# An embedding lookup with position add: hand-placed semaphores, 24 tile slots and stores in halves

## The chip, the cores and the metric

The kernel runs on one core of one Trainium2 chip. The metric is the device time in microseconds of one execution, as the median of ten. Its profile is one execution recorded by the hardware profiler.

## The reference

```python
batch, seq_len, vocab_size, d_model = 32, 512, 50000, 512
token_embed = embedding_table[indices]          # 32 x 512 rows of 512 float32
return (token_embed + position_embed).astype(np.float32)
```

For each of 32 sequences, 512 rows of 2048 bytes are picked from a table of 50,000 rows by an index, and row s of the position table is added to the row at place s. The result is 33.5 MB, and as much is gathered, so the work is almost wholly movement: about 67 MB through the DMA engines and one addition for each element.

## The kernel before

One sequence of 512 places is laid over 128 partitions, four places (k = 0 to 3) to a partition: place s = 4p + k stands in partition p. A whole sequence is then a tile of 128 x 4 x 512 float32, 1 MB, and each partition's part of it is 8192 contiguous bytes of the output.

The stages, by line:

- SyncE loads the indices of sequence 0 in their final layout (line 49, `idx0`), all indices with a sequence in each partition (line 51, `idx_raw`), and the position table in four parts (line 56, `pos_sb`).
- VectorE casts the indices to float32 (line 68), TensorE turns them with four small transposes (line 73), and VectorE casts them back into `idx_t` (line 75), which has the indices of all sequences with the place in the partition.
- ScalarE copies the position parts into PSUM (line 79, `pos_ps`).
- For each sequence `chunk` takes a tile, and for each k GpSimd issues an indirect DMA (line 88) that gathers 128 table rows, 256 KB, by one column of indices. VectorE adds the position part in place (line 94). When all parts of a tile are there SyncE stores it (line 97).

Sequences 0, 1 and 31 are cut into four tiles of one part with a store of 256 KB each; sequences 2 to 5 and 30 into two tiles with stores of 512 KB; the others are one tile with a store of 1 MB. That makes 46 stores and 128 gathers. The order on each engine is the order of this loop: GpSimd's queue holds only gathers after its first few instructions, VectorE's the additions, SyncE's the loads and then the stores.

The tile framework places all semaphores and waits. Its data pool has 20 tiles, each of the largest size, 8 KB a partition. It gives software DMAs (the gathers) eight semaphores in turn and hardware DMAs (loads and stores) eight others, so a gather waits for the eighth gather before it, and a store for the eighth hardware DMA before it. An instruction that needs more than one wait gets a semaphore instruction ahead of it. At the end of the program, at the launch line 132, SyncE waits for every one of these semaphores in ten semaphore instructions and a drain, and then all engines meet in a barrier.

Of the kernel before, what the change touches and what calls it, by code (L numbers as in the profile page):

```python
# [1 line left out]

# [4 lines left out]

P = 128
K = 4
BUFS = 20  # L10


@with_exitstack
def kernel(
    ctx: ExitStack,
    tc: tile.TileContext,
    indices: bass.AP,
    embedding_table: bass.AP,
    position_embed: bass.AP,
    out: bass.AP,  # L20
):

    nc = tc.nc
    f32 = mybir.dt.float32
    i32 = mybir.dt.int32
    add = mybir.AluOpType.add

    B, S = indices.shape
    V, D = embedding_table.shape
    assert S == P * K and B == 32  # L30
    assert V < (1 << 24), "an index passes through float32"


    idx_words = indices.bitcast(i32)
    idx_first = idx_words[0].rearrange("(p w) -> p w", p=P)
    out_rows = out.rearrange("b (p k) d -> b p k d", k=K)
    pos_rows = position_embed.rearrange("(p k) d -> p k d", k=K)
    table = embedding_table[:, :]

    const = ctx.enter_context(tc.tile_pool(name="const", bufs=1))  # L40
    data_pool = ctx.enter_context(tc.tile_pool(name="data", bufs=BUFS))
    psum = ctx.enter_context(
        tc.tile_pool(name="psum", bufs=1, space=bass.MemoryType.PSUM)
    )

    idx0 = const.tile([P, 2 * K], i32)
    nc.sync.dma_start(out=idx0[:], in_=idx_first)
    idx_raw = const.tile([B, S, 2], i32)  # L50
    nc.sync.dma_start(
        out=idx_raw[:], in_=idx_words.rearrange("b (s w) -> b s w", w=2)
    )
    pos_sb = [const.tile([P, D], f32, name=f"pos_sb{k}") for k in range(K)]
    for k in range(K):
        nc.sync.dma_start(out=pos_sb[k][:], in_=pos_rows[:, k, :])


    ones = const.tile([B, B], f32)
    nc.gpsimd.memset(ones[:], 1.0)  # L60
    ident = const.tile([B, B], f32)
    nc.gpsimd.affine_select(  # L62
        out=ident[:], in_=ones[:], pattern=[[-1, B]],
        compare_op=mybir.AluOpType.is_equal, fill=0.0, base=0,
        channel_multiplier=1,
    )
    idx_f = const.tile([B, P, K], f32)
    nc.vector.tensor_copy(  # L68
        out=idx_f[:].rearrange("b p k -> b (p k)"), in_=idx_raw[:, :, 0]
    )  # L70
    turned = psum.tile([P, K, B], f32)
    for k in range(K):
        nc.tensor.transpose(turned[:, k, :], idx_f[:, :, k], ident[:])  # L73
    idx_t = const.tile([P, K, B], i32)
    nc.vector.tensor_copy(out=idx_t[:], in_=turned[:])  # L75

    pos_ps = [psum.tile([P, D], f32, name=f"pos_ps{k}") for k in range(K)]
    for k in range(K):
        nc.scalar.copy(out=pos_ps[k][:], in_=pos_sb[k][:])  # L79

    def chunk(b, parts):
        at = 0
        for n in parts:
            data = data_pool.tile([P, n, D], f32, tag="data")
            for j in range(n):
                k = at + j
                where = idx0[:, 2 * k : 2 * k + 1] if b == 0 else idx_t[:, k, b : b + 1]
                nc.gpsimd.indirect_dma_start(  # L88
                    out=data[:, j, :],
                    out_offset=None,  # L90
                    in_=table,
                    in_offset=bass.IndirectOffsetOnAxis(ap=where, axis=0),
                )
                nc.vector.tensor_tensor(  # L94
                    out=data[:, j, :], in0=data[:, j, :], in1=pos_ps[k][:], op=add
                )
            nc.sync.dma_start(out=out_rows[b][:, at : at + n, :], in_=data[:])  # L97
            at += n

    for b in range(B):  # L100
        if b <= 1 or b == B - 1:
            chunk(b, (1, 1, 1, 1))
        elif b <= 5 or b == B - 2:
            chunk(b, (2, 2))
        else:
            chunk(b, (K,))


# [1 line left out]
_INS = ['indices', 'embedding_table', 'position_embed']  # L110
_OUTS = [((32, 512, 512), 'float32')]


# [23 lines left out]
```

## Time and profile before

| what | value |
|---|---|
| median of 10 runs | 184.56 us (184.51 to 184.64) |
| the profiled execution's own time | 184.57 us |
| its span, first to last instruction | 182.9 us |
| GpSimd busy | 121.7 us (67%), 134 instructions |
| VectorE busy | 87.3 us (48%), 130 instructions |
| gathers on GpSimd | 128, about 946 ns each |
| additions on VectorE | 128, 687 ns each |
| DMA moved | 68.33 MB, mean 374 GB/s over the span |

How to read it: a line of the page with one digit for each fortieth of the span gives the busy share in tenths. [...] data moves afterwards on the 16 DMA engines, which serve the gathers' queue (q0, software) and the loads' and stores' queue (q1, hardware) alike. SyncE computes nothing and only issues and waits; where an answer shows "SPq" it is SyncE's sequencer. The trace also has a record for each DMA packet, with start, duration and size, and for many of the semaphores' updates; where the text says packet records or landings, these are meant.

### The profile page before, as it was taken

Reading aid. Unit: us, or ns where it says so; the run is one execution under the profiler, and the core shown is the slowest. Engines: PE = TensorE matmul, PEld = TensorE weight load, DVE = VectorE, ACT = ScalarE, POOL = GpSimd, SP = SyncE. Lnnn points to the kernel's source line nnn. Section 1 sums busy time; section 2 is a strip of 40 time slices with the busy share of each in tenths; the row PEclk is TensorE's granted clock in tenths of the full one; section 3 lists DMA queues with packets and bytes.
Section 4 is the critical chain, followed back from the end, with each engine's and each line's share of the span. In section 5 each row is a group of like instructions: output and inputs, shape, how many; then the busy total and the mean of one; then the engine's idle time right before and its main releaser. Section 6 shows DMA issues by size and latency. Waiting matters only on the chain.

```text
span 182.9 us, 480 instructions
## 1 busy us (share of the span) xinstructions
PE 0.7 (0%) x4; PEld 0.6 (0%) x4; DVE 87.3 (48%) x130; ACT 3.6 (2%) x5; POOL 121.7 (67%) x134
## 2 busy tenths in 40 slices
PE   0100000000000000000000000000000000000000
PEld 0000000000000000000000000000000000000000
DVE  0163645545545454464746464464547465445300
ACT  2500000000000000000000000000000000000000
POOL 4777777777777777777777777778777777750000
DMA  4889999999999999999999999999999999999900
GB/s 129 319 258 369 358 395 390 418 398 410 400 391 398 403 407 410 406 416 404 418 413 412 417 410 419 409 414 419 416 420 407 417 414 417 411 409 417 396 15 0
DMA packets 17635, 68.33 MB, mean 374 GB/s; under 512 B 3008, under 2 KB 3008, under 8 KB 14560
## 3 DMA queue, kind: packets, MB, share of 16 engines
q0 software_dynamic: 10240, 33.56, 48.0%
q1 hardware_dynamic: 7392, 34.74, 46.5%
q14 instruction: 3, 0.02, 0.0%
HBM read 34.74 MB, written 33.55 MB: 373 GB/s over the span
## 4 chain that ended last, share of the span: by engine, by line
DMA 47%; POOL 22%; issue 18%; POOLq 3%; DVE 2%; SPq 1%; DVEq 1%
DMA data<-in_embedding_table_dram,idx_t 39%; POOL data L88 22%; DMA out_dram<-data 7%; POOLq L88 3%; DVE data L94 2%; SPq L97 1%; DMA idx<-in_indices_dram 1%; DVEq L94 1%
## 5 line engine op out<-in xcount | busy, mean ns | idle before, releaser
L88 POOL DMA_INDIRECT data<-in_embedding_table_dram,idx_t x124 | 117.2, 945 | 38.3 <-issue 38.0
L94 DVE TENSOR_TENSOR data<-data,pos_ps 128x512 f32<-128x512 f32 x128 | 86.6, 687 | 79.8 <-issue 54.1
L88 POOL DMA_INDIRECT data<-in_embedding_table_dram,idx x4 | 4.0, 994 | 2.4 <-DMA idx<-in_indices_dram 1.5
L79 ACT COPY pos_ps<-pos_sb 128x512 f32<-128x512 f32 x4 | 2.4, 589 | 4.2 <-DMA pos_sb<-in_position_embed_dram 4.0
L68 DVE CAST idx_f<-idx_raw 32x512 f32<-32x512 int32 x1 | 0.4, 415 | 3.8 <-DMA idx_raw<-in_indices_dram 3.8
L79 ACT ACT_TABLE_LOAD x1 | 1.3, 1283 | 0.8 <-PEq L121 0.8
L75 DVE CAST idx_t<-turned 128x128 int32<-128x128 f32 x1 | 0.3, 291 | 0.8 <-PE turned L73 0.8
L73 PE MATMUL turned<-ident,idx_f 32*128 32x32 f32 x4 | 0.7, 297 | 4.4 <-DVE idx_f L68 4.4
L73 PEld LDWEIGHTS turned<-ident,idx_f 32*128 32x128 f32 x4 | 0.6, 206 | 4.4 <-issue 4.4
L121 POOL MEMSET const-float32-0.0<- 128x1 f32 x1 | 0.1, 105 | 0.3 <-issue 0.3
L60 POOL MEMSET ones<- 32x32 f32 x1 | 0.1, 114 | 0.3 <-POOLq L121 0.3
L62 POOL TENSOR_SCALAR_AFFINE_SELECT ident<-ones 32x32 f32<-32x32 f32 x1 | 0.2, 202 | 0.1
L121 POOL MEMSET const-uint8-127<- 128x1 uint8 x1 | 0.1, 122 | 0.0
L121 POOL MEMSET const-bfloat16-1.0<- 128x1 bf16 x1 | 0.1, 116 | 0.0
L121 POOL MEMSET const-float32-1.0<- 128x1 f32 x1 | 0.1, 108 | 0.0
## 6 DMA issues: line engine op xcount, KB each, us to landing
out_dram<-data SPq DMA_DIRECT2D x24, 1024.0 KB
out_dram<-data SPq DMA_DIRECT2D x10, 512.0 KB
out_dram<-data SPq DMA_DIRECT2D x12, 256.0 KB
data<-in_embedding_table_dram,idx_t POOLq DMA_INDIRECT x124
pos_sb<-in_position_embed_dram SPq DMA_DIRECT2D x4, 256.0 KB
idx_raw<-in_indices_dram SPq DMA_DIRECT2D x1, 128.0 KB
data<-in_embedding_table_dram,idx POOLq DMA_INDIRECT x4
idx<-in_indices_dram SPq DMA_DIRECT2D x1, 4.0 KB
```

The lines of the kernel that those rows point to most:

```text
L60: nc.gpsimd.memset(ones[:], 1.0)
L62: nc.gpsimd.affine_select(out=ident[:], in_=ones[:], pattern=[[-1, B]], compare_op=mybir.AluOpType.is_equal, fill=0.0, base=0, channel_mul ...
L68: nc.vector.tensor_copy(out=idx_f[:].rearrange("b p k -> b (p k)"), in_=idx_raw[:, :, 0])
L73: nc.tensor.transpose(turned[:, k, :], idx_f[:, :, k], ident[:])
L75: nc.vector.tensor_copy(out=idx_t[:], in_=turned[:])
L79: nc.scalar.copy(out=pos_ps[k][:], in_=pos_sb[k][:])
L88: nc.gpsimd.indirect_dma_start(out=data[:, j, :], out_offset=None, in_=table, in_offset=bass.IndirectOffsetOnAxis(ap=where, axis=0),)
L94: nc.vector.tensor_tensor(out=data[:, j, :], in0=data[:, j, :], in1=pos_ps[k][:], op=add)
L97: nc.sync.dma_start(out=out_rows[b][:, at : at + n, :], in_=data[:])
L121: nc = _bacc.Bacc("TRN2", target_bir_lowering=False, num_devices=1)
```

## The change

The computation, the layout, the number of gathers and additions, and the order of gathers and additions stay. What changes:

- All instructions stand in one critical section, in which the framework places no waits; the kernel allocates its own semaphores and writes each wait. Entering it, every engine waits for a no-operation of SyncE; leaving it, SyncE signals the engines and collects a signal from each.
- The pool of 20 tiles becomes 24 fixed slots of one sequence each (`slots`), so sequence b uses slot b mod 24. Sequences 24 to 31 wait, at their first gather, for the stores of sequence b - 24.
- The gathers use 16 semaphores in turn (`LANES`), so a gather waits for the sixteenth before it.
- Each addition waits for its gather's semaphore, and those of sequence 0 also for the position copy. A store waits for one counter of additions, `s_add`, and no longer for an earlier DMA.
- Sequences 1 to 30 are stored in two halves of 512 KB; sequences 0 and 31 in four quarters of 256 KB. That makes 68 stores. The gathers of a sequence fill one slot, whatever the cut of its stores.
- SyncE ends with one wait for all stores of sequences 8 to 31 (`s_rest`). GpSimd ends with a drain inside the section.

The diff, cut to its core:

```diff
-BUFS = 20
+SLOTS = 24
+LANES = 16
+HALVES = (2, 2)
+QUARTERS = (1, 1, 1, 1)
...
+    slots = [sbuf(f"slot{n}", [P, K, D], f32) for n in range(SLOTS)]
...
+    stores = []
+    for b in range(B):
+        parts = QUARTERS if b in (0, B - 1) else HALVES
+        at = 0
+        for n in parts:
+            stores.append((b, at, n))
+            at += n
...
+    def rounds(g):
+        return 16 * (g // LANES + 1)
+
+    with tc.tile_critical(no_gpsimd_drain=True):
...
+        nc.gpsimd.wait_ge(s_first, 16)
+        for g in range(B * K):
+            b, k = divmod(g, K)
+            if g == K:
+                nc.gpsimd.wait_ge(s_idx, 1)
+            if b >= SLOTS and k == 0:
+                done = sum(1 for x in stores if x[0] == b - SLOTS)
+                nc.gpsimd.wait_ge(s_out[b - SLOTS], 16 * done)
+            where = idx0[:, 2 * k : 2 * k + 1] if b == 0 else idx_t[:, k, b : b + 1]
+            ins = nc.gpsimd.indirect_dma_start(
+                out=slots[b % SLOTS][:, k, :],
...
+            ).then_inc(s_gather[g % LANES], 16)
+            if g >= LANES:
+                ins._wait_ge(s_gather[g % LANES], rounds(g - LANES))
+        nc.gpsimd.drain()
...
+        for g in range(B * K):
+            b, k = divmod(g, K)
+            if b == 0:
+                nc.vector.wait_ge(s_ps, k + 1)
+            part = slots[b % SLOTS][:, k, :]
+            nc.vector.tensor_tensor(
+                out=part, in0=part, in1=pos_ps[k][:], op=add
+            )._wait_ge(s_gather[g % LANES], rounds(g)).then_inc(s_add, 1)
...
+        rest = 0
+        for b, at, n in stores:
+            done = s_out.get(b, s_rest)
+            rest += done is s_rest
+            nc.sync.dma_start(
+                out=out_rows[b][:, at : at + n, :],
+                in_=slots[b % SLOTS][:, at : at + n, :],
+            )._wait_ge(s_add, b * K + at + n).then_inc(done, 16)
+        nc.sync.wait_ge(s_rest, 16 * rest)
```

## The prediction

> **What bounds the kernel now.** I read the page's slices first, then the groups and queues, then a table of busy times by stretch, the gathers late in the order of time, and last the SyncE instructions of the launch line.
>
> The slices of the span (4.57 us each) and the DMA queues, from the page:
>
> ```profile
> DVE  0163645545545454464746464464547465445300
> ...
> POOL 4777777777777777777777777778777777750000
> DMA  4889999999999999999999999999999999999900
> GB/s 129 319 258 369 358 395 390 418 398 410 400 391 398 403 407 410 406 416 404 418 413 412 417 410 419 409 414 419 416 420 407 417 414 417 411 409 417 396 15 0
> ...
> q0 software_dynamic: 10240, 33.56, 48.0%
> q1 hardware_dynamic: 7392, 34.74, 46.5%
> ```
>
> The 16 DMA engines are full from the fifth slice to the 38th. q0 (gathers) and q1 (loads and stores) took 94.5% of the span, 172.8 us of all 16 engines. Then come two slices of nothing: 15 and 0 GB/s.
>
> The table by stretch (per engine busy us and instructions, then clock, DMA share, GB/s) shows the same closer:
>
> ```profile
> 36.00:44.00 8.00, 0.00 (x0) 0.00 (x0) 4.49 (x7) 0.00 (x0) 6.02 (x7) 1.00 1.03 408
> 48.00:60.00 12.00, 0.00 (x0) 0.00 (x0) 5.93 (x10) 0.00 (x0) 9.26 (x10) 1.00 1.00 394
> 60.00:80.00 20.00, 0.00 (x0) 0.00 (x0) 10.76 (x16) 0.00 (x0) 15.12 (x17) 1.00 1.01 408
> 80.00:160.00 80.00, 0.00 (x0) 0.00 (x0) 42.81 (x64) 0.00 (x0) 59.96 (x65) 1.00 1.02 414
> ...
> 174.60:182.90 8.30, 0.00 (x0) 0.00 (x0) 0.00 (x0) 0.00 (x0) 0.00 (x0) 1.00 0.00 0
> ```
>
> Share 1.02 is full: one packet per engine at every moment. From 174.6 to 182.9 nothing moves and nothing computes: 8.3 us, 4.5% of the span.
>
> GpSimd, in the order of time, with its gap in brackets:
>
> ```profile
> 159.70 0.95 POOL L88 DMA_INDIRECT data<-in_embedding_table_dram,idx_t  x1 [0.30 <-issue]
> 160.95 0.95 POOL L88 DMA_INDIRECT data<-in_embedding_table_dram,idx_t  x1 [0.30 <-issue]
> 162.20 0.95 POOL L88 DMA_INDIRECT data<-in_embedding_table_dram,idx_t  x1 [0.30 <-issue]
> ```
>
> A gather costs GpSimd 1.25 us, whatever it waits for. From the second gather (4.16) 126 steps of 1.25 us end at 161.66; the last one starts at 162.20. So all of its waits, for tiles and for the eighth gather back, cost 0.54 us in the whole run. GpSimd is a second bound a little below the DMA engines: 512 KB per 1.25 us is 419 GB/s, where the DMA moves 414.
>
> The launch line on SyncE (count, then minimum/median/maximum ns, first and last start):
>
> ```profile
> L132 SPq EVENT_SEMAPHORE  x12: 1/353/699, 175.7 to 182.8; - x12
> L132 SPq DRAIN  x3: 7/7/7, 182.0 to 182.3; - x3
> ```
>
> These are the framework's closing waits, ten instructions with up to two semaphores each, for every DMA lane. The last store's semaphore was complete at 174.53 by the trace's landings, yet SyncE reaches its drain at 182.04. In between most records lie 0.70 us apart, although the semaphores were satisfied. The final barrier takes 182.09 to 182.86. The last chain is thus: DMA engines full to 174.5, SyncE's slow wait list to 182.04, barrier.
>
> **What the Trainium skill says.** "DMA: Bandwidth & Descriptors", Rules for kernel authors, asks for 1 MiB or more per DMA for the most bandwidth. The trace agrees weakly: by its packet records a store packet of 8192 B (1 MB stores) takes 311 ns, of 4096 B (512 KB stores) 159 ns, of 2048 B 84 ns, so 26.3, 25.8 and 24.4 B/ns. The same page, Queues, rings and completion order, says that each engine takes turns between queue rows packet by packet. That fits a gather packet of 4096 B whose time varies with its neighbour: 170 ns from 28 to 46 us beside 4096 B stores, 164 from 100 to 160 beside 8192 B ones. [...] in the trace the first instructions follow the opening barrier by 0.07 us, branch included.
>
> **The change, part by part.** The sum is made against the profiled execution, 184.57 us with a span of 182.86, so 1.71 outside; it is within 0.01 of the median 184.56.
>
> 1. Entry. Each engine now runs one more branch that waits for a SyncE no-operation. By the 0.07 us above and one semaphore hop of some 0.05 (the barrier's release at 0.69 is seen at 0.74), about 0.2 us, on the path of the first index load. Bounds 0.1 and 0.6.
>
> 2. Gathers. 128 as before, now allowed 16 in flight and 24 tile slots instead of 20 tiles. All they can win on GpSimd is 0.54 us, and the DMA engines have no room for it: 0. The cover is that saturation: a gather lands 8.3 us after its issue (159.70 to 168.04), nearly seven in flight, so the limit of eight hardly held. Bounds: -0.5, and +0.5 if deeper queues cost.
>
> 3. Waits folded into instructions. DVE and SyncE lose separate semaphore instructions of 0.02 us when satisfied. Both engines have slack (DVE 48% busy). 0.
>
> 4. Stores in halves. Before: 12 of 256 KB, 10 of 512 KB, 24 of 1 MB, each of 128 rows of one packet: 1536 x 84 + 1280 x 159 + 3072 x 311 ns = 1288 us, over 16 engines 80.5. After: 8 of 256 KB and 60 of 512 KB: 1024 x 84 + 7680 x 159 = 1307 us, 81.7. That is +1.2, straight onto the bound. 22 more stores with 16 completion writes of 9 ns each add 22 x 9 ns = +0.2. The gather packets of the 24 sequences stored whole before (24 x 4 x 64 = 6144) may each take 6 ns more beside shorter stores: 6144 x 6 / 16 = +2.3. But part of that difference is drift along the run: at 46 to 60 us, beside 8192 B stores, they took 175. I take half, +1.1. Sum +2.5; bounds +1.2 (packet sums alone, some of it hidden) and +3.7. SyncE issues 22 more stores of 0.33 us, one per 2.5 us of data: covered. Sequence 1 in halves starts its stores a little later and the last sequence stays in quarters: 0.
>
> 5. Tail. Ten wait instructions go. SyncE waits once for all stores from sequence 8 on (the earlier ones are proved by slot reuse), then runs seven instructions (semaphore, drain, two semaphore waits, no-operation, branch, drain) and the same barrier. Before, from the last landing to the end: 182.86 - 174.53 = 8.33 us. After, if they run at their ordinary 0.02 to 0.07 us: landing seen 0.1, exit with two hops 0.5, barrier 0.77 = 1.4. The trace doesn't say why SyncE went slow from 167.3 on; if it does so again each instruction costs 0.70. I take 2.0, mostly fast with one slow step: -6.3. Bounds -6.9 and -2.0.
>
> Sum: 184.57 + 0.2 + 2.5 - 6.3 = 181.0 us. The DMA end moves from 174.5 to 177.2, the end of the span comes 2.0 later at 179.2.
>
> **The rivals.**
>
> - Slow SyncE follows (other side). Its 0.70 us steps began at 167.3, before the closing list, in ordinary stores and waits, so they may belong to SyncE late in the run and not to the list. Then eight instructions after the last landing cost 8 x 0.70 = 5.6, the barrier 0.77: 177.2 + 6.4 + 1.7 = 185.3. It decides when a step exceeds about 0.6 us. For it: the start before the list. Against: earlier SyncE waits took 0.017 us, and the run ends with fast steps after 182.
> - The half stores cost all they can: the rate stays at the 394 to 403 GB/s of the stretches from 28 to 60 us and never climbs to 414. For the 115 us up to 161 us 2.7% is 3.1 instead of the 2.5, at worst 5: 183.5 with the tail of 2.0. For it: 408 and 394 in the table. Against: the rate rises along the run with the stores' size unchanged.
> - Deeper queues win: early gathers no longer bunch, gather packets keep 164 ns, the tail takes its 1.4 us: 184.57 + 0.2 + 1.2 - 6.9 - 0.5 = 178.6. Against: share 1.02 leaves nothing to fill; only the first 20 us have some 3.7 us of idle share, and GpSimd's pace sets those.
> - The lanes don't do what they say: if GpSimd holds its own limit on outstanding gathers, 16 lanes act as eight. That changes nothing in the sum, 181.0.
>
> **How the numbers follow.** The forecast has a chance of 0.56 (lanes without effect included), deeper queues 0.08, costly halves 0.12, slow SyncE 0.20, and 0.04 for something that holds GpSimd up. Predicted 181.0. The range 178.6 to 185.1 holds the first three cases and the lower part of the slow one, leaving about 0.06 below and 0.14 above. A measurement here can tell 0.2%, 0.4 us, from no change. Faster takes the first three cases but for a sliver: 0.75; the slow case spreads about 185.3, with a quarter of it in the band: same 0.05, slower 0.20.
>
> **What would show it.** In the changed profile: the last DMA bytes near 177 and less than 2.5 us from there to the end of the span (step 5); store packets of 159 ns throughout q1 and gather packets between 164 and 170 (step 4); gathers still 1.25 us apart (step 2); the first index load at about 1.0 us instead of 0.81 (step 1). It is wrong if SyncE's last instructions again stand 0.7 us apart, or if the rate in the middle falls under 400 GB/s.

## The result and the profile after

The changed kernel takes 183.51 us (median of 8 runs, 183.41 to 183.59). The kernel before, measured beside it, takes 184.57. The ratio is 0.9942, with a 95% interval of 0.9934 to 0.9951, so the change wins 1.06 us. The forecast was 181.0, a win of 3.6: the direction was right, the size was not, and two terms of the sum were wrong by more than the whole effect.

The profiled execution of the changed kernel took 183.49 us, with a span of 182.3. First the slices and the queues of its page (a slice is 4.56 us here):

```profile
DMA  4889999999999999999999999999999999999800
GB/s 129 302 245 364 357 367 405 415 407 418 417 416 420 413 417 417 416 417 417 421 420 417 417 415 416 416 421 418 417 417 417 414 406 415 419 415 416 333 2 0
...
q1 hardware_dynamic: 10560, 34.74, 47.5%
q0 software_dynamic: 10240, 33.56, 46.9%
```

Then the same stretches as before, with the columns of the table by stretch (busy us per engine and instructions, clock, DMA share, GB/s):

```profile
48.00:60.00 12.00, 0.00 (x0) 0.00 (x0) 6.39 (x10) 0.00 (x0) 9.02 (x10) 1.00 1.03 417
60.00:80.00 20.00, 0.00 (x0) 0.00 (x0) 11.00 (x16) 0.00 (x0) 15.12 (x17) 1.00 1.03 416
80.00:160.00 80.00, 0.00 (x0) 0.00 (x0) 43.54 (x64) 0.00 (x0) 60.50 (x65) 1.00 1.03 417
...
172.00:174.60 2.60, 0.00 (x0) 0.00 (x0) 0.00 (x0) 0.00 (x0) 0.00 (x0) 1.00 0.16 61
174.60:182.30 7.70, 0.00 (x0) 0.00 (x0) 0.00 (x0) 0.00 (x0) 0.00 (x0) 1.00 0.00 0
```

Two things are to be seen. The rate in the middle did not fall with stores of half the size: it rose, from 394 to 417 GB/s at 48 to 60 us and from 414 to 417 at 80 to 160. The DMA engines are almost done at 172: their share in the next stretch is 0.16, where it was 0.70 in the kernel before:

```profile
172.00:174.60 2.60, 0.00 (x0) 0.00 (x0) 0.00 (x0) 0.00 (x0) 0.00 (x0) 1.00 0.70 269
```

Their last bytes move at 172.95, before at 174.54. And yet the stretch with nothing in it is still there, and longer: 182.3 - 172.95 = 9.3 us, before 8.3.

What fills it are SyncE's own records, on the line of the critical section (L89) and on the launch line (L189). The columns are count, then minimum/median/maximum ns, then first and last start in us:

```profile
L89 SPq EVENT_SEMAPHORE  x3: 17/1170/1400, 173.9 to 176.6; - x3
L89 SPq NOP  x2: 4/8/13, 0.8 to 178.7; - x2
...
L189 SPq DRAIN  x3: 15/700/704, 179.4 to 182.2; - x3
L189 SPq EVENT_SEMAPHORE  x2: 5/10/15, 182.2 to 182.3; - x2
```

The list is short now: from the last bytes on, SyncE has eleven records up to the final barrier's last. The first three, up to 173.96, are quick. The next ones take 1.17, 1.40, 0.70 and 0.70 us, or stand 0.7 to 2.6 us apart, until 182.2; then three in a row pass in 0.05 us. In the trace of before the slow steps ended at 181.99, and they had begun at 167.3 among the stores (SyncE's store line from 165 us on):

```profile
L97 SPq DMA_DIRECT2D out_dram<-data x5: 332/556/706, 165.7 to 174.3; - x5
L97 SPq EVENT_SEMAPHORE  x4: 17/695/700, 166.0 to 172.9; - x4
```

The DMA engines finished 1.6 us earlier, and SyncE became quick within 0.25 us of the same moment.

The balance of the two profiled executions: last bytes -1.6, from there to the end of the span +1.0, outside the span 1.71 to 1.2, -0.5. Sum -1.1, the measured change.

### The profile page after: what moved, and what is told of

The parts are those of the page before. It is cut to its first block, busy times and chain, and to the rows that moved or that the text cites. A ratio compares the mean times of both kernels' runs of the same rounds, so it can differ in the third digit from the quotient of the medians.

```text
span 182.3 us, 421 instructions
## 1 busy us (share of the span) xinstructions
PE 0.7 (0%) x4; PEld 0.6 (0%) x4; DVE 88.3 (48%) x130; ACT 3.6 (2%) x5; POOL 121.9 (67%) x134
## 4 chain that ended last, share of the span: by engine, by line
POOL 63%; issue 23%; DMA 5%; DVE 2%; POOLq 1%; SPq 0%
POOL slot L116 63%; DMA slot<-in_embedding_table_dram,idx_t 4%; DVE slot L146 2%; DMA idx<-in_indices_dram 1%; POOLq L124 1%; POOLq L114 0%; SPq L189 0%; SPq L89 0%
## 5 line engine op out<-in xcount | busy, mean ns | idle before, releaser
L116 POOL DMA_INDIRECT slot<-in_embedding_table_dram,idx_t x124 | 117.2, 945 | 37.8 <-issue 37.8
L146 DVE TENSOR_TENSOR slot<-slot,pos_ps 128x512 f32<-128x512 f32 x128 | 87.6, 687 | 77.1 <-issue 39.4
L116 POOL DMA_INDIRECT slot<-in_embedding_table_dram,idx x4 | 4.1, 1027 | 2.4 <-DMA idx<-in_indices_dram 1.5
```

The source lines that it names most:

```text
L116: ins = nc.gpsimd.indirect_dma_start(out=slots[b % SLOTS][:, k, :], out_offset=None, in_=table, in_offset=bass.IndirectOffsetOnAxis(ap=whe ...
L146: nc.vector.tensor_tensor(out=part, in0=part, in1=pos_ps[k][:], op=add)._wait_ge(s_gather[g % LANES], rounds(g)).then_inc(s_add, 1)
```

## The experiments

Each kernel is the changed one with the edit shown, but for the fourth of the first group, which is the kernel before with an edit. "Timed" means in three rounds beside the kernel before, which took 184.74 us for the first timed group and 184.81 for the second; the others were run once. Every run, timed or not, was recorded. The tail is the time from the last DMA bytes to the end of the span.

### First: does SyncE's load make it slow, and what do the half stores cost?

**Half of the work.** Sequences 16 to 31 are left out: 64 gathers instead of 128.

```diff
-    for b in range(B):
+    N = 16
+    for b in range(N):
...
-        for g in range(B * K):
+        for g in range(N * K):
...
```

> Leaves out sequences 16 to 31 altogether (their rows of the output are not written); the changed kernel otherwise. The question is the idle end, 9.3 us from the last DMA bytes (172.95) to the end of the span (182.3). If SyncE's slow steps belong to the end of its own program whatever went before, the end stays at 9 us and the span is 172.95 - 16 x 2.51 + 9.3 = about 142 - wait for 64 gathers of 1.25 us less = 80 us less, so 102 us. If they come with the amount of work done before (a backlog of some kind that grows along the run), the end shrinks to about half, 4 to 5 us, and the span to 97 us.

Measured: 97.22 us, span 95.5, last bytes at 93.70. The tail is 1.8 us, and no SyncE instruction is slow: its closing instructions on the launch line take 7 and 17 ns each. So the short list is worth what step 5 said, in a run that is half as long. The slow SyncE comes with something that grows along the run.

**Stores issued from ScalarE**, and the wait for the last ones with them. SyncE keeps only 20 instructions.

```diff
-            nc.sync.dma_start(
+            nc.scalar.dma_start(
...
-        nc.sync.wait_ge(s_rest, 16 * rest)
+        nc.scalar.wait_ge(s_rest, 16 * rest)
```

> Stores and the wait for them move from SyncE to ScalarE; SyncE keeps the six loads and the section's entry and exit. If an engine that has issued the stores is slow afterwards, SyncE is now fast and the end falls from 9.3 to about 2 to 3 us: 176 to 177 us. If SyncE is slow at the end for a reason of its own, the end stays above 7 us and the time between 182 and 184.

Measured, timed: 182.52 us, ratio 0.9877 (0.986 to 0.9893), last bytes at 173.69. It is the fastest version that does all the work. SyncE on the launch line:

```profile
L189 SPq DRAIN  x3: 7/379/700, 174.3 to 177.6; - x3
L189 SPq EVENT_SEMAPHORE  x2: 700/1047/1394, 175.5 to 179.0; - x2
```

After a wait of 2.95 us its first two records at 174.3 are quick (13 and 7 ns); the next ones take 0.38 to 1.39 us, with 0.7 us between one and the next, though SyncE had done almost nothing all run. So its own stores didn't make it slow. The span ends at 178.9 to 179.7 in the four runs, yet their times lie within 0.13 us of each other, 2.8 to 3.6 us after the span's end: something other than the last recorded instruction ends this program.

**Stores whole**, in the sizes that the kernel before used; the rest is as in the changed kernel.

```diff
-        parts = QUARTERS if b in (0, B - 1) else HALVES
+        parts = QUARTERS if b <= 1 or b == B - 1 else HALVES if b <= 5 or b == B - 2 else (K,)
```

> The changed kernel with the stores cut as before the change (46 stores, most of 1 MB). If the half stores shortened the gather packets (165 ns instead of 169 over the run), they go back to 164 to 167 in the middle, the last DMA bytes move from 172.95 to about 174.5 and the time to 185. If the slots and lanes did it, the packets stay at 159 to 160 and the time stays at 183.5 or falls by the 1.4 us of longer stores' cheaper packets.

Measured, timed: 183.77 us, ratio 0.9945 (0.9928 to 0.9961). The stretches:

```profile
80.00:160.00 80.00, 0.00 (x0) 0.00 (x0) 43.07 (x64) 0.00 (x0) 60.49 (x65) 1.00 1.02 414
160.00:172.00 12.00, 0.00 (x0) 0.00 (x0) 6.16 (x9) 0.00 (x0) 2.44 (x3) 1.00 1.02 415
172.00:174.60 2.60, 0.00 (x0) 0.00 (x0) 0.00 (x0) 0.00 (x0) 0.00 (x0) 1.00 0.72 276
```

With whole stores the rate is back at 414 and the share of the stretch before 174.6 at 0.72, as in the kernel before; the gather packets in the middle take 164 ns again and the last bytes move at 174.62. So it is the cut of the stores, and not the lanes or the slots, that brings the DMA engines' end forward. By how much varies: 1.7 us against this profile of the changed kernel, but three other versions with halves (stores, closing, or both on ScalarE) end at 173.5 to 173.7, about 1 us before whole stores. And that is worth 0.3 us at most (183.77 against 183.51, the intervals overlap), since SyncE is slow until 182.4 in this kernel too. The expectation of about 185 missed for that reason.

**Halves in the kernel before.** Its own structure, with the stores of sequences 1 to 30 in halves.

```diff
-        if b <= 1 or b == B - 1:
+        if b == 0 or b == B - 1:
...
-        elif b <= 5 or b == B - 2:
-            chunk(b, (2, 2))
         else:
-            chunk(b, (K,))
+            chunk(b, (2, 2))
```

> The kernel before with sequences 1 to 30 in halves, framework waits and all, 20 tiles of the pool now each half filled. If the half stores alone make the gather packets shorter, its last DMA bytes come at about 173 (before: 174.5) and its time is 183.0 plus what more closing waits cost, so about 183. If the hand-placed section made them shorter, the last bytes stay at 174.5 or later and the time at 184.6 to 186.

Measured, timed: 187.83 us, ratio 1.017 (1.0153 to 1.0187), slower than before, and more than either answer had it. The store line on SyncE and the stretches:

```profile
L97 SPq DMA_DIRECT2D out_dram<-data x68: 3/689/1395, 9.4 to 182.2; - x68
L97 SPq EVENT_SEMAPHORE  x66: 3/689/1395, 10.5 to 182.1; - x66
```

```profile
80.00:100.00 20.00, 0.00 (x0) 0.00 (x0) 11.52 (x17) 0.00 (x0) 15.12 (x17) 1.00 1.03 415
100.00:140.00 40.00, 0.00 (x0) 0.00 (x0) 21.34 (x33) 0.00 (x0) 30.25 (x33) 1.00 1.02 399
140.00:180.00 40.00, 0.00 (x0) 0.00 (x0) 16.02 (x24) 0.00 (x0) 17.38 (x19) 1.00 0.85 334
```

Here each store is two instructions on SyncE, a wait and the issue, and the median record of both is 0.69 us; the slow ones begin at about 50 us. Up to 100 us the transfers are as good as in the changed kernel (415 GB/s); then SyncE can't issue stores fast enough, the share falls to 0.85 and the last bytes move at 183.84. Folding the wait into the store, which the prediction put at nothing, is then what lets the changed kernel issue 68 stores without this. That is read from the trace: no run folds the waits alone.

### Second: who is made slow, and until when?

The theory now was that each gather leaves a piece of hidden work behind, 1.40 us of it where gathers are issued every 1.25, and that SyncE's instructions crawl until it is worked off: at 2.9 + 128 x 1.40 = 182.1 us. The rivals: it is the time since the start, SyncE's role in the closing, or the amount of data.

**Three quarters of the work.** Sequences 24 to 31 are left out: 96 gathers. The edit is that of the half, with N = 24.

> Leaves out sequences 24 to 31 (their rows are not written). In all full runs so far SyncE's slow steps end at about 182 us, whenever the DMA ends, and with 64 gathers there were none. A gather theory: something that SyncE shares with the gathers takes 1.40 us a gather, two steps of 0.70, while gathers come every 1.25, so that the backlog is gone 2.9 + 128 x 1.40 = 182.1 us after the start. With 96 gathers it is gone at 2.9 + 134.4 = 137.3; the DMA ends at about 133, SyncE's steps are slow up to 137.3 and the span is 138. If the slow end is as long in every run that is long enough, it lasts 9 us here too: span 142. If it grows with the time beyond some 95 us for another reason, something between 135 and 142 that fits neither.

Measured: 140.39 us, span 138.4, last bytes at 132.85. SyncE on the line of the section, then on the launch line:

```profile
L90 SPq EVENT_SEMAPHORE  x3: 17/702/1389, 133.5 to 136.8; - x3
L90 SPq NOP  x2: 3/8/13, 0.8 to 137.5; - x2
...
L190 SPq DRAIN  x3: 7/7/10, 137.5 to 137.8; - x3
L190 SPq EVENT_SEMAPHORE  x2: 17/17/17, 137.7 to 138.4; - x2
```

Slow (1.39, 0.70) until 137.52, quick from there. The gathers give 2.9 + 96 x 1.40 = 137.3. In the half the same sum gives 92.5, before its last bytes at 93.70, and nothing was slow. So the two ends that were seen, 137.52 and 182, lie on one line; the half agrees with it but marks no end.

**The section closed by ScalarE**, with the wait for the last stores on it; the stores stay on SyncE.

```diff
-    with tc.tile_critical(no_gpsimd_drain=True):
+    with tc.tile_critical(
+        sync_engine=mybir.EngineType.Activation, no_gpsimd_drain=True
+    ):
...
-        nc.sync.wait_ge(s_rest, 16 * rest)
+        nc.scalar.wait_ge(s_rest, 16 * rest)
```

> Stores stay on SyncE; the wait for them and the section's closing waits move to ScalarE. If only SyncE is slow and each of its steps costs 0.70, its remaining ones (two semaphore waits, three drains, two barrier waits) still take 5 us or more: 181 to 183. If it is the closing waits themselves that are slow on any engine, ScalarE takes them slowly and the time stays at 183.5. If SyncE has room for some steps before it goes slow, 178 to 180.

Measured, timed: 182.85 us, ratio 0.9895 (0.9878 to 0.9911). The launch line of ScalarE and that of SyncE, the same kinds in the same stretch of the run:

```profile
L191 ACTq DRAIN  x2: 8/8/8, 174.7 to 175.3; - x2
L191 ACTq EVENT_SEMAPHORE  x2: 17/17/17, 175.2 to 178.2; - x2
...
L191 SPq DRAIN  x3: 698/700/1398, 175.3 to 180.8; - x3
```

ScalarE's take 8 to 17 ns, and its closing waits before them, at 174.3 to 174.6, took 17 to 38. SyncE's were quick up to 174.85 too; from 175.25 on they take 0.70 or 1.40 each until the end of the span at 182.3. So SyncE is hit and ScalarE is not. The final barrier needs every engine, so the end stays where SyncE puts it.

**All of it on ScalarE**: stores, wait and closing (both edits above together).

> Stores, the wait for them and the section's closing waits on ScalarE; SyncE has the six loads and its share of the final barrier, eight instructions. If SyncE alone is slow, this leaves it the fewest steps: the end falls under 4 us and the time to 177 to 180 us. If any engine that closes the section is slow, it stays at 182.5 like the run with the stores alone on ScalarE.

Measured, timed: 182.91 us, ratio 0.9898 (0.9882 to 0.9915); 177 to 180 had been expected, a miss. SyncE has eight instructions left after 174 and needs them until 181.1. Taking work off SyncE shortens nothing further. The four runs of this kernel have spans of 181.1 to 182.5 and times within 0.23 us, as with the stores on ScalarE: the time hardly follows the last recorded instruction. Three layouts of the closing give 182.5, 182.9 and 182.9.

**Plain loads from ScalarE** in place of the gathers: consecutive table rows, so no row is looked up.

```diff
-            ins = nc.gpsimd.indirect_dma_start(
-                out=slots[b % SLOTS][:, k, :],
...
+            ins = nc.scalar.dma_start(
+                out=slots[b % SLOTS][:, k, :], in_=table[g * P : (g + 1) * P, :]
+            ).then_inc(s_gather[g % LANES], 16)
```

> Leaves out the lookup: the 128 gathers on GpSimd are replaced by 128 plain loads of 128 consecutive table rows, issued from ScalarE; bytes, additions, stores and waits are the same. If SyncE's slow steps come from the gathers, there are none: the end is under 2.5 us from the last bytes. If they come with the stores, the additions or the amount of DMA, the end is 7 us or more as in the changed kernel.

Measured: 178.78 us, span 177.1, last bytes at 174.80; the tail is 2.3 us and no SyncE instruction is slow, at a run length of 177 us. Time since the start is not the cause.

### Third: what of a gather leaves the work behind?

**Half the rows.** Gathers, adds and stores on partitions 0 to 63 only, half the output left out.

```diff
-            where = idx0[:, 2 * k : 2 * k + 1] if b == 0 else idx_t[:, k, b : b + 1]
+            where = idx0[0:64, 2 * k : 2 * k + 1] if b == 0 else idx_t[0:64, k, b : b + 1]
...
-                out=slots[b % SLOTS][:, k, :],
+                out=slots[b % SLOTS][0:64, k, :],
...
```

> Each gather, addition and store covers partitions 0 to 63 alone (the other half of the output is not written): 128 gathers of 64 rows. If the hidden work is a fixed 1.40 us a gather instruction, SyncE is slow until about 182 us as before although the DMA ends near 166, and the span is 182 to 183. If it goes with the rows (0.70 us for 64), it is done with the gathers at 164 and the end is under 2.5 us: span 168 or less.

**Half of each row.** Gathers fetch 1024 B instead of 2048 (half the columns are left out of adds and stores too).

```diff
-    table = embedding_table[:, :]
+    table = embedding_table.rearrange("v (h d) -> (v h) d", h=2)
...
-                out=slots[b % SLOTS][:, k, :],
+                out=slots[b % SLOTS][:, k, 0 : D // 2],
...
```

> Each gather picks 128 half rows of 1024 B, and additions and stores cover 256 columns (half of the output is not written, and the rows are others, since an index now counts half rows): the same number of gathers and rows, half the bytes. If the hidden work goes with the bytes moved, SyncE is not slow at the end: span 168 or less. If it goes with gathers or rows, SyncE is slow until about 182: span 182 to 183.

Measured: 184.8 us with half the rows and 182.42 with half of each row, where half the data is moved and the last bytes come at 167.54 and 167.62. SyncE with half of each row, section line, then launch line:

```profile
L89 SPq EVENT_SEMAPHORE  x3: 17/704/1398, 168.6 to 171.0; - x3
...
L189 SPq DRAIN  x3: 700/700/1400, 173.8 to 178.7; - x3
L189 SPq EVENT_SEMAPHORE  x2: 698/699/700, 177.3 to 180.1; - x2
```

It crawls to the end of the span at 180.8, and with half the rows to 183.2. Neither run shows when the slow stretch would have ended, and 183.2 is 1.1 us past the 182.1 of the theory. With half the rows a few instructions at 176.2 to 176.4 were quick, after a wait of several us, and the next ones slow again, as with the stores on ScalarE: a pause buys a few quick steps. By the theory's two answers, slow steps until about 182 or none, the hidden work goes neither with the rows nor with the bytes of a gather; what is left is their number.

**Gathers paced.** Two small fills of a scratch tile behind each gather on GpSimd, to stretch its step above 1.40.

```diff
+            for n in range(2):
+                nc.gpsimd.memset(pace[:, 2 * g + n : 2 * g + n + 1], 1.0)
```

> Two small fills on GpSimd after each gather, of a scratch tile that nothing reads, so that gathers come further apart. If a gather's hidden work of 1.40 us piles up only because gathers come every 1.25 us, then with 1.45 us or more between gathers nothing piles up: the end after the last bytes is under 2.5 us, and the span is 2.9 + 128 x the new distance + about 12. If the slow end has to do with the number of gathers and not with their distance, it is 7 us or more.

Measured: 193.25 us, span 191.5, last bytes at 189.34. The fills fit into the gap and the step stayed at 1.25; but then GpSimd itself was held up. From its order of time (start, us, operation, idle before it in brackets):

```profile
30.75 0.95 POOL L117 DMA_INDIRECT slot<-in_embedding_table_dram,idx_t  x1 [0.16 <-issue]
31.69 0.15 POOL L126 MEMSET pace<- 32x1 f32 x2
32.00 0.95 POOL L117 DMA_INDIRECT slot<-in_embedding_table_dram,idx_t  x1 [0.16 <-issue]
32.94 0.12 POOL L126 MEMSET pace<- 32x1 f32 x1
33.33 0.09 POOL L126 MEMSET pace<- 32x1 f32 x1 [0.27 <-issue]
34.23 0.94 POOL L117 DMA_INDIRECT slot<-in_embedding_table_dram,idx_t  x1 [0.82 <-issue]
35.42 0.09 POOL L126 MEMSET pace<- 32x1 f32 x1 [0.24 <-issue]
36.12 0.09 POOL L126 MEMSET pace<- 32x1 f32 x1 [0.61 <-issue]
37.04 0.94 POOL L117 DMA_INDIRECT slot<-in_embedding_table_dram,idx_t  x1 [0.83 <-issue]
```

Nothing recorded holds the gathers at 34.23 and 37.04 ("issue"). Over the run 24 of the 127 steps are longer than 1.3 us, most of them 2.1 or 2.8, three or four times 0.70; between them some dozen steps of 1.25 go by. The mean from 3.05 to 180.67 is 177.6 / 127 = 1.40 us: the rate that the theory gave the hidden work, now seen on the engine that issues. And since GpSimd was held to it, nothing was left over at the end: SyncE's closing instructions at 190.2 to 191.5 are quick (7 to 28 ns). The fills have a share in the hold-up, which the run doesn't separate, so the run bears out the rate less cleanly than it was built to.

**Plain loads from GpSimd**: the loads of consecutive rows again, now on the gathers' engine and queue.

```diff
-            ins = nc.gpsimd.indirect_dma_start(
-                out=slots[b % SLOTS][:, k, :],
...
+            ins = nc.gpsimd.dma_start(
+                out=slots[b % SLOTS][:, k, :], in_=table[g * P : (g + 1) * P, :]
```

> Leaves out the lookup: 128 plain loads of 128 consecutive table rows issued from GpSimd in place of the gathers. If the hidden work belongs to any DMA that GpSimd makes descriptors for, SyncE is slow at the end here too, until 2.9 us + 128 x its price. If it belongs to indirect ones alone, the end is under 2.5 us.

Measured: 173.68 us, span 172.0, last bytes at 169.75. SyncE:

```profile
L89 SPq EVENT_SEMAPHORE  x3: 17/28/28, 170.6 to 170.8; - x3
L89 SPq NOP  x2: 13/13/13, 0.8 to 170.9; - x2
...
L185 SPq DRAIN  x3: 7/7/7, 171.0 to 171.3; - x3
L185 SPq EVENT_SEMAPHORE  x2: 17/17/17, 171.2 to 171.9; - x2
```

No slow step, with the same number of DMAs on the same engine, a mean step of 1.13 us. So it is the indirect form, not GpSimd or its queue. The run is 9.8 us shorter than the changed kernel, but that is not the price of the hidden work, since its issues are cheaper too. An estimate for that price takes the changed kernel's last bytes at 172.95, the tail of 2.3 us of the plain loads from ScalarE and 1.7 us outside the span, as both runs with plain loads have it: 177, so about 6.5 us less than measured.

### What follows from them together

In these recorded runs the span of the kernels before and after ends when a rate of 1.40 us per gather, from the first gather on, has been served, and not when the transfers end. Four counts of evidence: the moment moves with the number of gathers (137.5 for 96, 182 for 128, nothing left over for 64); SyncE is still slow at 180.8 and later where the transfers end 7 us earlier (the two runs with half the data), and the moment stays where they end 1.6 earlier (the change); the slow steps are gone with plain loads from either engine; and where gathers were held to 1.40 on the average they are gone too. Stores, SyncE's load and the closing's layout move the time by a microsecond, down to the version with the stores on ScalarE.

What the hidden work is stays open, and one rival above all is left: that it is work of the recording. No run was made without recording, but three things in the traces speak for this rival.

**Order.** SyncE's drains on the launch line carry its signals for the two rounds of the last barrier, in the changed kernel recorded from 180.81 and from 182.25 on. GpSimd waits for these signals, and its semaphore instructions show that it had both earlier, the first at 178.77 and the second at 180.87:

```profile
L189 POOLq EVENT_SEMAPHORE  x4: 17/17/17, 178.8 to 180.9; - x4
```

With plain loads from GpSimd the order is the natural one, signal at 171.06 and wait over at 171.10. With the stores on ScalarE, GpSimd and ScalarE are through the last barrier, which needs SyncE too, at 175.3, and yet SyncE's records go on to 179.7 and the run took 182.54. In the kernel before, the packets of the last store start at 173.10 and its issue is recorded at 174.29. And among the stores of the kernel before in halves there are issues of 3 to 14 ns, where an undisturbed one takes 332.

**Loss.** With plain loads, from either engine, the trace has 3232 records of the DMAs' steps of their semaphores, 16 for each of 202 DMAs. In the changed kernel, with as many DMAs, it has 443, and in the half of the work 322 of 1696.

**Pace.** The steps that are recorded in the changed kernel between 40 and 160 us come a median of 0.70 us apart, the step of SyncE's slow records; with plain loads from GpSimd it is 0.03.

So a slow record of SyncE is late, and its length is not the time that its instruction took. SyncE was held up all the same: GpSimd, done with its own drain at 174.03, had SyncE's first signal only at 178.77. A recording that gathers fill up, and that SyncE has to wait for, would do all this. That isn't shown either; if it is so, part or all of the 1.40 us per gather, and of the times here, is a price of recording.

That 4096 B gather packets are shorter beside 4096 B stores is shown; why is not. Fewer and larger gathers weren't tried: an indirect gather here takes one index per partition.

## Why the prediction was right or wrong

- **Step 1, entry, +0.2: right.** The first index load starts at 1.02 us instead of 0.81. The 0.07 us from which it was worked out had no branch in it that the trace of before records; in the changed kernel the branch is recorded, with 33 ns on SyncE.
- **Step 2, gathers and lanes, 0: right.** They are 1.25 us apart in all 123 steps of the main group, the last at 161.98 where it was 162.20. The same 1.25 was read as a second bound just below the DMA engines. It was the visible part of one: 1.40 per gather already set the end of the recorded run, and nothing in the 1.25 says so.
- **Step 3, waits folded in, 0: right in the sum, for a reason that fails.** The cover named was SyncE's slack. SyncE had none late in the run, where its records stand 0.70 us apart. With 68 stores and separate waits the kernel before loses 3.1 us (187.83 against 184.74). By that trace, the fold is the condition under which halves cost nothing.
- **Step 4, halves, +2.5: the wrong sign.** The last bytes came 1.6 us earlier with the entry's 0.2 in it, so -1.8 in this profile, and about -1 by the three other versions with halves. The terms for the stores were roughly right (4096 B packets took 160 ns). The term for the gathers was not: +6 ns, half of it taken, where 165 became 160 (mean at 60 to 140 us). The 170 ns beside 4096 B stores had been read at 28 to 46 us in the trace of before. In the changed kernel the same stretch, with the same neighbours, has 163, so the 170 were not the neighbour's price; what made them isn't shown. The prediction saw a drift and halved the term, where it should have asked for its sign. The Trainium skill's advice in "DMA: Bandwidth & Descriptors", Rules for kernel authors, 1 MiB or more per DMA, did not decide here: 512 KB stores gave 417 GB/s, 1 MB stores 414.
- **Step 5, tail, -6.3: the step that failed.** From the last bytes to the end of the span it was 9.3 us and not 2.0, so the term was +1.0. The tail was taken to be as long as its list of instructions; the runs show that it lasts until the gathers' 1.40 us each are served, at about 182, however short the list. The list was shortened as said, and in runs without slow steps the tail is 1.8 to 2.3 us (half the work, plain loads), so the price of the instructions was right. But "mostly fast with one slow step" was a guess about a cause that the trace didn't give. The trace had the clue: the slow steps began at 167.3 in ordinary stores, so they didn't belong to the list. This went into a rival at 0.20 instead of into the forecast.
- **The sum.** Step 4 was 4.3 us too high and step 5 was 7.3 too low; with the 0.5 us outside the span, which was not forecast, the result lies 2.5 above 181.0. That it is no further off is luck, since the two errors have opposite signs, and so is the right direction, since the shorter tail that it was to come from didn't come.
- **The rival "slow SyncE follows"** had half of the mechanism, that the slow steps don't belong to the list. It priced it per instruction, 8 x 0.70 after the DMA end. The runs show an end that stands still at about 182: with a DMA end of 172.95, 1.6 us earlier, the tail just grew. Together with step 4's wrong +2.5 this rival said 185.3, slower than before; with the measured DMA end its own sum is 172.95 + 6.4 + 1.7 = 181.1.
- **The rivals on costly halves and deeper queues** fell: the rate didn't stay at 394 to 403 GB/s, and the first 20 us did not fill (302 and 245 GB/s in slices 2 and 3).
- **Where the 1.06 us come from.** With whole stores in the new structure 0.97 of it is there already, so it belongs to the section with its short list; about half of it lies outside the span, where 1.71 became 1.2 us. What ends the time there isn't shown. The rest lies in the span: before, 0.87 us of drains and barrier followed the last slow record (181.99 to 182.86), now 0.05 us do. The expected gain of 6 us from the shorter list and a gain of 1 to 1.7 us in the transfers, which had not been expected, both ended in the wait for the gathers' hidden work.

## What to carry to other kernels

Where satisfied waits take long at the end of a program, look for when that began and what it scales with (leave out a half and a quarter of the work) before you price a shorter list of them: the list may be the clock that shows the bound and not the bound. A recorded run of many small indirect gathers can have a bound of its own, per gather instruction, that neither the gathers' busy time nor the DMA share shows; whether an unrecorded run has it is open here. Before you price a slow record, look at what needs its outcome: where another engine's wait is over, or a store's packets move, before the record begins, the record is late. And where an engine is slow, each instruction on it counts: 68 stores with separate waits cost 3 us here, and moving the issues to another engine gained 1.

## What the runs showed of the hardware

All of this is of recorded runs.

- 128 x 2048 B indirect gathers from GpSimd are issued every 1.25 us (0.95 busy), but something behind them is served at 1.40 us per gather (ends at 137.52 with 96 gathers and at 181.99 to 182.4 with 128). With half the rows or half the bytes SyncE is slow at 180.8 and later as well. Plain loads of the same size from GpSimd took 0.54 us busy and a mean step of 1.13.
- While it lags, SyncE's records take 0.70 us or multiples of it, satisfied waits and drains of 7 to 28 ns among them, and come after their effects (by 2.1 us for a barrier's signal); after a pause of some us a few pass at the ordinary price. ScalarE's closing instructions at the same time took 8 to 17 ns.
- With indirect gathers most of the semaphores' steps are missing from the trace (443 of 3232 recorded), with plain loads none.
- A time can lie well past the last recorded instruction: 1.7 us in the kernel before, 2.8 to 3.6 with the stores on ScalarE.
- Stores of 4096 B packets beside gathers of 4096 B packets: 160 ns each at 60 to 140 us; beside stores of 8192 B the gathers' took 164 to 165.
